# Forgetting values by four query tiles in one bank, low probabilities by half-width products: one change to a hybrid decoder trunk

## The chip, the cores and the metric

The kernel runs on one core of a Trainium2 chip. The metric is the device time of one execution in microseconds (us), taken as the median of several. TensorE is called PE in the profile (its weight loads PEld), VectorE DVE, ScalarE ACT, GpSimd POOL, and SP is the queue that issues the transfers.

## The reference

Two layers work on 1024 tokens of 1024 channels, in float32. Layer 0 mixes by pooling over windows of 2, 4, 8 and 16 tokens and by a 4-head attention into 256 memory tokens. Layer 1 uses the same kind of memory attention beside a "forgetting" attention with 16 heads of 64 channels. Each layer ends in an output projection and a layer norm. The change is about the forgetting attention:

```python
def shared_kv(x, w_kv_shared, b_forget):
    h = x @ w_kv_shared
    k = h[..., :D_MAIN]...; v = h[..., D_MAIN:2 * D_MAIN]...
    log_f = jax.nn.log_sigmoid(h[..., 2 * D_MAIN:] + b_forget)
    return k, v, jnp.cumsum(log_f, axis=1)

# for each block of 128 queries
logits = jnp.einsum('bqhd,bkhd->bhqk', qi, k) * scale
logits = logits + (ci[..., :, None] - cum_k[:, :, None, :])
p = jax.nn.softmax(jnp.where(mask, logits, -jnp.inf), axis=-1)
out = jnp.einsum('bhqk,bkhd->bqhd', p, v)
```

## The kernel before

Products in float32 precision are made of parts. A projection ("slab", 128 output channels by 1024 tokens) takes for each of its two halves of 512 tokens 24 products: 8 blocks of input channels by three terms, high by high and twice high by low. Each half accumulates in one PSUM bank and is then read by ACT and DVE (`evac`). `slab` is a generator that gives up control after each product (line 213), so that its products can be used as filling between others. PSUM has eight banks here: `pj` 3 (slabs), `L` 2 (logits), `T` 2 (exponentials and transposes), `O` 1 (values). PE's order is written out by hand (`manual_schedule(engines={PE})`); the other engines' order comes from a scheduler.

The **forgetting attention** (`fox`) goes over 16 heads, and in each over 8 query tiles of 128 queries from the last (i = 7, with 1024 keys) to the first (i = 0, with 128 keys): 128 steps. A step does this:

- `probs` (lines 789 to 818): the logits of the tile in one or two parts of up to 512 keys, two products each, in an `L` bank (line 197). DVE adds the gates' row R and takes the running extreme (line 807), ACT makes the exponentials into a `T` bank (line 815).
- `halves` (lines 833 to 838), one step later: ACT makes float16 high probabilities (line 836), DVE the low ones (line 837).
- `turn` (line 846): one transposing transfer turns both halves of the tile, into a tile of its own out of the pool of six `T` tiles in SBUF.
- `values`, LAG = 5 steps later and for two query tiles together (every second step): for each tile i and key block j one product with high and one with low probabilities, both with the stationary 128 x 128 tile that holds 64 columns of V's high part and 64 of its low part. Both tiles accumulate in the one `O` bank. ACT (line 862) and DVE (line 863) then add the two halves of partitions and scale.
- `pair_out` (lines 868 to 874): after the second head of a pair POOL multiplies the output by the gate in four pieces and SP writes it to memory (`y1d`).
- `fill.pump`: filling (projections of the next pair of heads, gates) by a budget. `SHARE` says how the filling that is left is spread over the eight steps of a head; before, it is even.

Ahead of `fox`, `start_units` interleaves the first pair's K and Q slabs (`own`) with the projection of the first values and of the gates' logits (`v_first`, line 685), the chain of small DVE operations for the gates (`forget_gates`: cumulative sum by products in lines 716 and 718, a transpose in line 722, a write of the rows to memory), and the next pair's slabs (`following`). `forget_rows` reads a row of gates back for each head.

`mem_kv` makes keys and values of the memory: eight projections for each layer, each of 24 products with 256 columns into a `pj` bank; their weights are split into high and low parts by `split_w`. With `low[0]` set that is done by POOL alone (lines 162 to 164), otherwise by ACT and DVE (lines 154, 155, 159).

`OutProj` is the output projection: `open` takes four banks for two token tiles, `products` (line 442) gives its products, `norm` (lines 489 to 507) reads the banks. Its first part (`early`) is filling at the end of `fox`.

## Time and profile before

| | |
|---|---|
| median of three runs | 1231.65 us (1231.56 to 1234.4) |
| the profiled execution | 1232.92 us, its span 1231.2 us |
| mean granted clock of PE | 0.996 |
| busy: PE / DVE / ACT / POOL | 1205.1 / 800.0 / 709.0 / 226.2 us |
| values products of the forgetting attention | 1152, busy 75.1 us |
| forgetting attention | about 653 to 1115 us of the span |

Busy time of PE is the union of its matmuls with modelled ends; matmuls overlap, so a mean length (220 ns) is longer than the time from one start to the next. In a table of stretches each engine has its busy us and, in brackets, the number of its instructions; then come the granted clock, the transfer engines' share and GB/s. In the list of waits stand the total us, the count and the longest. In a row of groups stand the busy time, the mean ns of one, and the idle time just ahead with what ended it.

### The profile page before, as it was taken

What the parts mean: (1) busy time and instruction counts of PE and PEld (TensorE: products, weight loads), DVE (VectorE), ACT (ScalarE), POOL (GpSimd) and SP (SyncE); (2) the same over time, 40 slices, a digit from 0 to 9 for tenths busy, and PEclk for the clock granted to TensorE, in tenths of its full rate; (3) what the DMA queues carried; (4) which work ended last, traced back from release to release, by engine and by line L of the source; (5) the groups of instructions that cost most, each with busy time, mean ns of one, the idle gap of its engine ahead of it and who ended that gap; (6) DMA issues with size and microseconds to landing.
All of it is one profiled execution on the core that took longest, in us unless ns stands there. A gap on an engine that the chain in (4) does not pass through costs nothing. (4 is left out here: it accounts for less than half of the span.)

```text
span 1231.2 us, 20033 instructions
## 1 busy us (share of the span) xinstructions
PE 1205.1 (98%) x7018; PEld 762.4 (62%) x7018; DVE 800.0 (65%) x1901; ACT 709.0 (58%) x1495; POOL 226.2 (18%) x360
## 2 busy tenths in 40 slices
PE   8999999999999999999998999999999999999996
PEld 4567665555556657566775666666666666655553
DVE  6544776376555458267455888778877888775643
ACT  7566765373532238477334777767776777785210
POOL 2000000000000000000003444444434434550000
PEclk9999999999999999999999999999999999999998
DMA  6333443232453335234516678878777888996430
GB/s 226 117 103 95 120 122 136 94 120 95 144 193 117 103 103 188 61 87 110 184 41 158 143 175 184 185 161 193 172 175 180 179 181 201 229 218 203 165 109 35
DMA packets 267414, 178.68 MB, mean 145 GB/s; under 512 B 212272, under 2 KB 225712, under 8 KB 267312
## 3 DMA queue, kind: packets, MB, share of 16 engines
q1 hardware_dynamic: 267312, 177.40, 53.7%
q8 instruction: 55, 0.90, 0.3%
q14 instruction: 47, 0.39, 0.1%
HBM read 94.97 MB, written 22.61 MB: 96 GB/s over the span
## 5 line engine op out<-in xcount | busy, mean ns | idle before, releaser
L213 PE MATMUL pj<-A,w 128*128 128x512 bf16 (+1 forms) x2928 | 698.7, 393 | 1.9 <-ACT A L154 1.0
L213 PEld LDWEIGHTS <-w 128*128 128x128 bf16 x1984 | 175.4, 98 | 213.2 <-issue 42.7
L213 PEld LDWEIGHTS pj<-A,w 128*128 128x128 f32 x976 | 179.5, 189 | 44.5 <-ACT A L154 2.6
L815 ACT ACTIVATE T<-MK,s 128x512 f32<-128x512 f32 x192 | 110.7, 577 | 49.2 <-DVE s L807 37.3
L837 DVE SCALAR_TENSOR_TENSOR P<-T,s,P 128x512 f16<-128x512 f32 x192 | 111.7, 613 | 33.3 <-ACT P L836 31.6
L836 ACT ACTIVATE P<-T,s 128x512 f16<-128x512 f32 x192 | 102.6, 576 | 50.5 <-issue 21.1
L155 DVE TENSOR_TENSOR w<-raw,w 128x512 bf16<-128x512 f32 x106 | 74.3, 702 | 83.5 <-PE pj L213 50.4
L442 PEld LDWEIGHTS <-T 128*128 128x128 bf16 x736 | 70.8, 98 | 86.6 <-issue 3.7
L197 PE MATMUL L<-B,B 128*128 128x512 f32 (+3 forms) x384 | 109.1, 387 | 7.6 <-DVE s L807 6.7
L157 POOL TENSOR_SCALAR A<-A 128x512 bf16<-128x512 f32 (+1 forms) x20 | 17.4, 884 | 464.4 <-ACT A L154 464.4
L197 PEld LDWEIGHTS L<-B,B 128*128 128x128 f32 x384 | 70.3, 189 | 35.5 <-DVE s L807 18.0
L154 ACT CAST w<-raw 128x512 fp32r<-128x512 f32 x106 | 65.4, 617 | 36.1 <-PE pj L213 25.1
L807 DVE CUSTOM_DVE_ANT_0 MK<-L,R 128x512 f32<-128x512 f32 (+3 forms) x128 | 72.8, 569 | 10.8 <-PE L L197 3.7
L197 PEld LDWEIGHTS <-V 128*128 128x128 f16 x1152 | 67.5, 98 | 18.1 <-issue 8.2
L197 PE MATMUL O<-T,V 128*128 128x128 f16 x1152 | 75.1, 220 | 1.6 <-DVE G L863 1.0
L155 DVE TENSOR_TENSOR T<-T,T 128x1024 bf16<-128x1024 f32 x23 | 28.1, 1221 | 73.7 <-ACT T L154 36.8
L163 POOL TENSOR_TENSOR w<-raw,w 128x512 bf16<-128x512 f32 x54 | 70.1, 1298 | 24.4 <-PE pj L213 22.8
L799 POOL TENSOR_SCALAR_AFFINE_SELECT R<-R 128x128 f32<-128x128 f32 x128 | 41.1, 327 | 163.4 <-DVE s L807 131.4
L159 ACT CAST w<-w 128x512 bf16<-128x512 f32 x106 | 65.6, 618 | 7.2 <-PE pj L213 5.6
L159 ACT CAST T<-T 128x1024 bf16<-128x1024 f32 (+1 forms) x39 | 37.0, 957 | 42.0 <-PE L L442 35.6
L154 ACT CAST T<-T 128x1024 fp32r<-128x1024 f32 x23 | 24.1, 1047 | 53.0 <-DMA T<-y1d 26.9
L442 PE MATMUL pj<-B,T 128*128 128x512 bf16 (+1 forms) x186 | 48.7, 392 | 0.0
(238 smaller groups left out, 1698.8 us busy)
## 6 DMA issues: line engine op xcount, KB each, us to landing
raw<-in_win_dram SPq DMA_DIRECT2D x96, 256.0 KB, 2.8
raw<-in_wout_dram SPq DMA_DIRECT2D x40, 256.0 KB, 2.9
B<-B SPq DMA_DIRECT2D x32, 256.0 KB, 4.2
R<-cumd SPq DMA_DIRECT2D x16, 512.0 KB, 4.2
y0d<-Y SPq DMA_DIRECT2D x12, 512.0 KB, 2.6
T<-y0d SPq DMA_DIRECT2D x12, 512.0 KB, 3.8
T<-y1d SPq DMA_DIRECT2D x11, 512.0 KB, 3.8
raw<-in_wmk_dram SPq DMA_DIRECT2D x16, 256.0 KB, 2.6
```

The lines of the kernel that those rows point to most:

```text
L154: pin(nc.scalar.copy(hi, src))
L155: pin(nc.vector.tensor_tensor(lo[0], src, hi.bitcast(F32), ALU.subtract))
L159: nc.scalar.copy(lo[1], hi.bitcast(F32))
L163: nc.gpsimd.tensor_tensor(lo[0], src, hi.bitcast(F32), ALU.subtract)
L197: nc.tensor.matmul(acc, a, b, start=i == 0, stop=i == len(terms) - 1)
L213: nc.tensor.matmul(acc, a, b, start=start, stop=stop)
L442: nc.tensor.matmul(acc, y, w, start=c == 2 and j == firsts[id(acc)], stop=c == 1 and j == lasts[id(acc)])
L799: nc.gpsimd.affine_select(R[:, qs], R[:, qs], [[-1, P]], ALU.is_ge, -NEG, base=0, channel_multiplier=1).ins
L807: nc.vector.tensor_tensor_reduce(p[:, lo:up], lg, R[:, lo:up], 1.0, top, ALU.add, ALU.min, m[:, n : n + 1])
L815: nc.scalar.activation(e, p[:, lo:up], AF.Exp, bias=top, scale=-1.0, accum_out=sums[:, n, hd % 2, i : i + 1],)
L836: nc.scalar.activation(pair[:, lo:up], e, AF.Copy, scale=r)
L837: nc.vector.scalar_tensor_tensor(pair[:, L + lo : L + up], e, r, pair[:, lo:up], ALU.mult, ALU.subtract)
```

## The change

- `values` takes four query tiles (i = 7 to 4, then 3 to 0) together, in one `O` bank of 512 columns. First come all high products as before; then all low products, with a stationary tile of only the 64 columns of V's high part, whose result goes in turn to partitions 0 to 63 and 64 to 127. The product of low probabilities with V's low part is no longer formed. Each bank is begun once (`start` on the first product only). The number of products and of weight loads on PE stays the same (7010 and 4873).
- The turned probabilities of a head lie in five tiles in place of eight (`HOMES`). `pair_out` gives up control after each piece and is continued step by step, all four pieces after the head's last call.
- PSUM: `L` 3, `pj` 2. The products of the pooling map take `L`; the output projection's banks go by a list in turn.
- `SHARE` is uneven: (1.4, 3.1, 2.9, 2.6, 1.6, 2.2, 2.1, 1.9).
- `start_units`: 24 products of `own` ahead of `v_first` in place of 48; 27 in place of 33 between the last transposes of V and the cumulative sum; nine after it in both; then 60 in place of 30 ahead of the first logits.
- In layer 1, the second half of each memory projection's weights is split by POOL.

```diff
-SHARE = (1,1,1,1,1,1,1,1)
+SHARE = (1.4, 3.1, 2.9, 2.6, 1.6, 2.2, 2.1, 1.9)
+HOMES = ((4, 14), (3, 10), (4, 8), (4, 0), (3, 0), (2, 0), (1, 0), (0, 0))
...
-    def slab(pieces_dram, XH, XL, evac, banks=("pj", 3)):
+    def slab(pieces_dram, XH, XL, evac, banks=("pj", 2)):
...
             for pc in range(2):
+                low[0] = l == 1 and pc == 1
                 a, b = split_w(w_dram[pc], [P, 4, P])
+                low[0] = False
...
-        def open(self, banks=(("pj", 3),) * 2 + (("L", 2),) * 2):
-            accs = [ps([P, NH], *bank) for bank in banks]
+        def open(self, sp):
+            pj, l, t, o = ("pj", 2), ("L", 3), ("T", 2), ("O", 1)
+            turned = ((pj, pj, l, l), (t, t, l, o)) if self.l else ((pj, pj, l, l), (l, o, pj, pj), (l, l, l, o))
+            accs = [ps([P, NH], *bank) for bank in turned[sp % len(turned)]]
...
-                    acc = ps([P, NH], "pj", 3)
+                    acc = ps([P, NH], "L", 3)
...
-            yield from islice(own, 48)
+            yield from islice(own, 24)
             yield from v_first()
             gates = forget_gates()
             next(gates)
             for _ in v_turned():
                 yield from islice(own, 6)
+            yield from islice(own, 27)
+            next(gates)
+            yield from islice(own, 9)
+            next(gates)
             yield from own
-            yield from islice(following, 9)
-            next(gates)
-            yield from islice(following, 9)
-            next(gates)
-            yield from islice(following, 30)
+            yield from islice(following, 48)
...
-                lg = ps([P, NH], "L", 2)[:, : up - lo]
+                lg = ps([P, NH], "L", 3)[:, : up - lo]
...
-            pt[hd, i] = T([P, 2 * ST, P], F16)
-            nc.sync.dma_start_transpose(pt[hd, i][:, :n, :], two[:, : n * P])
+            home, at = HOMES[i]
+            if at == 0:
+                homes[home] = T([P, 2 * ST, P], F16)
+            pt[hd, i] = homes[home][:, at : at + n, :]
+            nc.sync.dma_start_transpose(pt[hd, i], two[:, : n * P])
...
-            acc = ps([P, 2 * P], "O", 1)
-            for i in (2 * c, 2 * c + 1):
-                mm3(
-                    acc[:, (i % 2) * P : (i % 2) * P + P],
-                    [
-                        (v[:, b, 2 * j : 2 * j + 2, :].rearrange("p e d -> p (e d)"), pt[hd, i][:, e * (i + 1) + j, :])
-                        for j in range(i + 1) for e in range(2)
-                    ],
-                )
+            acc = ps([P, NH], "O", 1)
+            blocks = [(i, j) for i in range(4 * c + 3, 4 * c - 1, -1) for j in range(i + 1)]
+
+            def cols(i):
+                return slice((i % 4) * P, (i % 4 + 1) * P)
+
+            for n, (i, j) in enumerate(blocks):
+                nc.tensor.matmul(
+                    acc[:, cols(i)], v[:, b, 2 * j : 2 * j + 2, :].rearrange("p e d -> p (e d)"), pt[hd, i][:, j, :],
+                    start=n == 0, stop=False, skip_group_check=True,
+                )
+            for n, (i, j) in enumerate(blocks):
+                half = slice(64 * (n % 2), 64 * (n % 2) + 64)
+                nc.tensor.matmul(
+                    acc[half, cols(i)], v[:, b, 2 * j, :], pt[hd, i][:, i + 1 + j, :],
+                    start=False, stop=n >= len(blocks) - 2, skip_group_check=True,
+                )
...
-            oc = o[own, c * 2 * P : (c + 1) * 2 * P]
+            oc = o[own, c * NH : (c + 1) * NH]
...
-        def pair_out(pr, c, o, g):
-            for k in {1: (3, 2, 1), 0: (0,)}.get(c, ()) if g is not None else ():
+        def pair_out(pr, o, g):
+            for k in (3, 2, 1, 0) if g is not None else ():
                 cols = slice(k * 2 * P, (k + 1) * 2 * P)
                 nc.gpsimd.tensor_tensor(o[:, cols], o[:, cols], g[:, cols], ALU.mult)
-            if c == 0:
-                nc.sync.dma_start(y1d[pr // 4, :, pr % 4, :], o)
+                yield
+            nc.sync.dma_start(y1d[pr // 4, :, pr % 4, :], o)
...
-                    if older and older[1] % 2 == 0:
-                        values(older[0], older[1] // 2, older[2])
-                        if older[0] % 2:
-                            pair_out(older[0] // 2, older[1] // 2, older[2], gs.get(older[0] // 2))
+                    if older and older[1] % 4 == 0:
+                        values(older[0], older[1] // 4, older[2])
+                        if older[0] % 2 and older[1] == 0:
+                            finished = pair_out(older[0] // 2, older[2], gs.get(older[0] // 2))
+                    next(finished, None)
```

More of the change, by code (lines that the diff above doesn't have):

```diff
@@ L469, in rest @@
                 if c == 2:
-                    accs[sp] = self.open((("T", 2), ("T", 2), ("pj", 3), ("O", 1))) if 0 in accs and sp == 1 else self.open()
+                    accs[sp] = self.open(sp)
                 src, (yh, yl) = T([P, 4, 2 * P], F32), halved(T, [P, 4, 2 * P])
@@ L559, in slab_of @@
                     first[d] if g == 0 else win[0, 2 * g + d], XH, XL,
-                    lambda cols, acc: nc.scalar.copy(us[d][:, cols], acc), ("L", 2) if g == 0 and d == 1 else ("pj", 3),
+                    lambda cols, acc: nc.scalar.copy(us[d][:, cols], acc), ("L", 3) if g == 0 and d == 1 else ("pj", 2),
                 )
@@ L640, in trunk_kernel @@
         flog = fg[:, 0, :]
+        tr = G((P, 2, P))
+        tri, ones = tr[:, 0, :], tr[:, 1, :]
+        nc.gpsimd.memset(ones, 1.0)
+        nc.gpsimd.affine_select(tri, ones, [[1, P]], ALU.is_ge, 0.0, base=0, channel_multiplier=-1)
         def values_of(u):
@@ L678, in v_first @@
             for s in range(ST):
-                acc = ps([P, NH], "pj", 3)
+                acc = ps([P, NH], "pj", 2)
                 terms = []
```

15 lines of the change are left out of this document (6 added, 9 removed).

## The prediction

> **What bounds the kernel now.** I read the page's first part, then the busy time by stage, then what TensorE waits for, then the groups and the order of TensorE's instructions around the forgetting attention.
>
> ```profile
> span 1231.2 us, 20033 instructions
> PE 1205.1 (98%) x7018; PEld 762.4 (62%) x7018; DVE 800.0 (65%) x1901; ACT 709.0 (58%) x1495; POOL 226.2 (18%) x360
> ```
> ```profile
> core 0: us, PE busy (x) PEld busy (x) DVE busy (x) ACT busy (x) POOL busy (x), PEclk, DMA share, GB/s
> ...
> 450.00:480.00 30.00, 27.82 (x200) 21.53 (x200) 24.34 (x53) 19.91 (x40) 1.23 (x2) 1.00 0.42 144
> ...
> 653.00:664.00 11.00, 7.90 (x28) 4.10 (x27) 5.28 (x14) 4.07 (x9) 3.19 (x6) 0.84 0.85 215
> 664.00:780.00 116.00, 114.62 (x745) 75.67 (x744) 94.69 (x277) 84.99 (x204) 51.16 (x86) 1.00 0.74 165
> 780.00:900.00 120.00, 119.15 (x799) 79.67 (x798) 96.01 (x280) 84.94 (x199) 52.78 (x86) 1.00 0.80 185
> 900.00:1000.00 100.00, 99.39 (x667) 66.28 (x664) 80.79 (x234) 73.24 (x171) 41.81 (x70) 1.00 0.75 172
> 1000.00:1030.00 30.00, 27.96 (x181) 17.32 (x179) 23.46 (x73) 21.85 (x54) 10.81 (x20) 1.00 0.96 193
> 1030.00:1115.00 85.00, 83.73 (x523) 53.60 (x522) 65.36 (x160) 63.94 (x138) 42.15 (x58) 1.00 0.91 225
> ```
> ```profile
> PE L L197 <- DVE s L807: 6.7, 13, 2.9
> PE pj L197 <- DVE s L501: 1.6, 1, 1.6
> ...
> PE O L197 <- DVE G L863: 1.0, 2, 0.7
> ...
> PE O L197 <- DMA T<-P: 0.6, 1, 0.6
> ```
>
> TensorE is busy for 98% of the span: the time is the length of its own stream plus a few holes. Only two things can move it: a shorter stream, or fewer holes. The holes that the change can reach are 2.2 us in 450:480 (the second layer's memory keys), 3.1 us in 653:664 with a granted clock of 0.84 (the first forgetting tiles), and in 664:1115, the forgetting attention, (1.38 + 0.85 + 0.61 + 2.04 + 1.27) = 6.2 us. Most of them are waits of the logits for the vector engine to read a bank (6.7 us in 13 waits). DVE is busy there for 360 of 451 us (0.80): it is next in line, but not the bound.
>
> **The values products: the main term.**
>
> ```profile
> L197 PE MATMUL O<-T,V 128*128 128x128 f16 x1152 | 75.1, 220 | 1.6 <-DVE G L863 1.0 <-DMA T<-P 0.6
> ...
> L197 PEld LDWEIGHTS <-V 128*128 128x128 f16 x1152 | 67.5, 98 | 18.1 <-issue 8.2 <-DMA T<-P 1.4
> ```
> ```profile
> 700.80 1.85 PE L197 MATMUL O<-T,V 128*128 128x128 f16 x30
> ```
>
> One call of 30 products takes 1.85 us, of which the last one's own length is 0.22: (1.85 - 0.22) / 29 = 56 ns from start to start. All 1152 make 64.5 us of stream. The changed kernel still issues 1152. The 576 with high probabilities stay as they are. The 576 with low probabilities use a 64-column stationary tile and write partitions 0 to 63 and 64 to 127 in turn; they take 576 x 56 ns = 32.3 us now. No instruction in this trace uses half the array's columns, so I bound it.
>
> Lower end: two neighbours in different halves run side by side, and a pair takes 56 ns: 288 x 56 ns = 16.1 us go. Upper ends: the halves run one after the other, 0 us; or the weight load shows. The nearest rows for a load that sets the pace are the f32 products with little to stream:
>
> ```profile
> 642.36 0.46 PE L716 MATMUL O<-G,G 128*128 128x128 f32 x2 [0.87 <-DVE G L708]
> 642.66 1.63 PE L718 MATMUL O<-G,G 128*128 128x112 f32 x14
> 644.14 2.10 PE L213 MATMUL pj<-A,w 128*128 128x512 bf16 x9
> 646.57 0.33 PE L722 MATMUL T<-ident,G 128*128 128x128 f32 x1 [0.32 <-DVE G L719]
> 646.73 6.78 PE L213 MATMUL pj<-A,w 128*128 128x512 bf16 x30
> 653.15 1.28 PE L197 MATMUL L<-B,B 128*128 128x512 f32 x4
> 654.27 2.22 PE L213 MATMUL pj<-A,w 128*128 128x512 f32 x9
> 659.39 0.73 PE L197 MATMUL L<-B,B 128*128 128x512 f32 x2 [2.90 <-DVE s L807]
> ```
> ```profile
> L718 PEld LDWEIGHTS O<-G,G x14: 192/192/193, 642.5 to 644.0; 128*128 128x128 f32 x14
> ```
>
> Those 14 have streams of 112 columns down to 16 and still go at (1.63 - 0.26) / 13 = 105 ns each: a slow 128-column load. If the 64-column loads cost that much, (105 - 56) x 576 = 28 us come on top; if half as much, 53 ns each, loads in series keep 56 ns and nothing is won. I take 65 ns a pair, so 288 x (112 - 65) = -13.5, rounded to **-13 us**. It lies near the lower end because today's loads of 98 ns already hide completely behind a pitch of 56: the nearest row has more than one load under way.
>
> The Trainium skill (TensorEngine Tiling (Array Packing), Key Properties) says that different tiles load and multiply in parallel, which by itself gives the -16; its section Restrictions says that column tiling switches the fast weight load off, which is the case of 53 ns by the row above. No run here shows either yet.
>
> Going from full-width products to half-width ones and back happens twice in each of the 32 calls: 64 changes. No such change is in the trace. Its price lies between 0 and an emptied array with a bare load: a product alone lasts 220 ns in place of 56, and the load is 98, so at most 0.26 us each or 16.8 us. I take 0.08, half of the 164 ns of the emptying, as the rows show no stop where f16 and f32 follow each other: **+5 us**. The skill's same section says that a change of the tiling mode drains TensorE, which speaks for a price above 0.
>
> Half as many calls also mean 32 evacuations of 512 columns in place of 64 of 256, and the O bank is asked for every fourth step, not every second. That saves DVE and ACT some busy time off the path; the 1.0 us wait for L863 belongs to the holes below. The transposes of probabilities keep their number; only their tiles are packed, and each is still read four or more steps after its issue (128 steps in 451 us: 14 us).
>
> **The start.** Before, 30 products of projection stand between the gates' transpose (646.57) and the first logits; these then wait 2.9 us for their bank, since the vector engine starts on them only when the row of gates has come. The clock falls to 0.84 over 11 us, worth 1.8 us. After, 60 products (60 x 6.78 / 30 = 13.6 us) lie there, and DVE's first logits came 12.1 us after that transpose:
>
> ```profile
> 646.22 0.29 DVE L719 COPY G<-O 128x128 f32<-128x128 f32 x1
> ...
> 658.63 0.69 DVE L807 CUSTOM_DVE_ANT_0 MK<-L,R 128x512 f32<-128x512 f32 x1 [2.45 <-DMA R<-cumd]
> ```
>
> So 3.1 + 1.8 go. But ahead of the cumulative sum (642.36, which already waits 0.87) stand 27 products in place of 33, 1.3 us less cover: **-3.5 us**, between -4.9 and -1.
>
> **Holes in the forgetting attention.** Three logits banks let the logits run one bank further ahead, and SHARE gives the steps with long rows more projection work. Of 6.2 us I take **-3.5**; ends -6.2 and 0, since DVE still has to read all the logits.
>
> **Memory keys, layer 2.** Half the weight splits go to POOL:
>
> ```profile
> L163 POOL TENSOR_TENSOR w<-raw,w 128x512 bf16<-128x512 f32 x54 | 70.1, 1298 | 24.4 <-PE pj L213 22.8 <-PE L L197 0.7
> L162 POOL TENSOR_SCALAR w<-raw 128x512 fp32r<-128x512 f32 x54 | 33.9, 628 | 78.1 <-DVE G L704 43.9 <-PE pj L213 25.6 <-issue 8.6
> L164 POOL TENSOR_SCALAR w<-raw 128x512 bf16<-128x512 f32 x54 | 33.4, 618 | 0.0
> ```
> ```profile
> 480.89 0.41 DVE L290 TENSOR_REDUCE s<-pj 128x1 f32<-128x256 f32 x1
> ...
> 480.90 4.27 PE L197 MATMUL pj<-T,w 128*128 128x256 bf16 x36
> ...
> 484.60 0.48 DVE L298 SCALAR_TENSOR_TENSOR MK<-pj,s,MK 128x256 f16<-128x256 f32 x1
> ```
>
> POOL needs 0.63 + 1.30 + 0.62 = 2.5 us for one, TensorE 24 x 4.27 / 36 = 2.8 us for one projection: POOL keeps up, DVE loses eight subtractions, and the 2.2 us of waits mostly go. Against it stands the third slab bank: the projection read at 480.89 is released at 485.1, while two banks want it back one projection after 480.90, at 483.7. That is 1.4 us, and perhaps as much again for the next. I take **-1**, between -2.2 and +2. In the forgetting stage a slab's half lasts 24 products of 0.22 us (6.78 us for 30 at 646.73) with other work between, so two slab banks are covered there; in the first layer likewise.
>
> **The end.** Pair 7's four gatings run behind the last call, where before one did:
>
> ```profile
> 1108.57 0.73 POOL L872 TENSOR_TENSOR G<-G,G 128x256 f32<-128x256 f32 x1 [4.90 <-DVE G L863]
> ```
> ```profile
> 1109.33 0.33 SPq L874 DMA_DIRECT2D y1d<-G  x1
> ...
> 1112.79 0.52 SPq L472 DMA_DIRECT2D T<-y1d  x1
> ```
> ```profile
> 1120.28 1.04 ACT L154 CAST T<-T 128x1024 fp32r<-128x1024 f32 x1 [3.62 <-DMA T<-y1d]
> ```
> ```profile
> 1125.46 0.81 PE L442 MATMUL pj<-R,T 128*128 128x512 f32 x2
> ```
>
> The write moves 3 x 0.73 = 2.2 us later, and behind it on SP's queue the last weight fetches, the norm's rows and the read of pair 4 to 7. That read's high half is ready at 1121.3 and used at 1125.5: 4.1 us hide it, so **0**, at worst +2 if TensorE gets there sooner.
>
> **Sum.** The profiled execution took 1232.9 us (span 1231.2 and 1.7 around it): 1232.9 - 13 + 5 - 3.5 - 3.5 - 1 = 1216.9. The median of the runs shown lies 1.3 below that execution: **1216 us**.
>
> **Rivals.** (1) The loads set the pace: low products stay at 56 ns, the rest as above: 1231.65 - 3 = 1229. For it: the 105 ns of L718, halved. Against: the loads of two halves touch different columns. Chance 0.15.
>
> (2) Slower: the halves work one after the other and the array empties at every change of width, 64 x 0.26 = +16.8 against -8 from start, holes and keys: 1240. It needs both parts; with no gain from the halves it decides from 8 / 64 = 0.125 us per change, with the gain of 13 never below 0.33. For it: a lone product lasts 220 ns. Against: nothing in the trace stops at a change of type. This is also the case in which the change does not do what it says. Chance 0.16.
>
> (3) DVE takes over: its 360 us stand in a stage that shrinks from 451 to 439 us (0.82), and half of that stage's net gain of 11.5 returns as waits of logits for L807: 1222. For it: those waits are already the largest. Against: SHARE fills those steps. Chance 0.12.
>
> **How the numbers follow.** The forecast has 0.57. All lower ends together give -16.1 - 4.9 - 6.2 - 2.2 = -29.4, so 1202; all of them at once is unlikely, and the range starts at 1204. Above, it must take in rival 1 and most of rival 2: 1238. About 0.3%, 3.7 us, is what a measurement here can tell from no change, so faster means below 1228. Faster: the forecast, rival 3 and half of rival 1, less a little for a dear drain: 0.74. Same: the other half of rival 1: 0.09. Slower: rival 2: 0.17.
>
> **What would show it.** Right: low products at 28 to 40 ns from start to start, so that the group of values products falls from 75 to about 62 us; no 2.9 us wait at the first logits and a clock of 1.00 there; L807 waits below 3 us. Wrong: low products at 56 ns or more, holes of 0.1 to 0.3 us where the width changes, new waits for pj banks at the memory values or at the late gates, or a longer wait than 2.2 us for L708.

## The result, and the profile after

The kernel with the change takes 1236.65 us (median of 20 runs, 1233.63 to 1239.59), the one before 1234.22 us (20 runs, 1231.25 to 1236.83). The ratio is 1.0022, with a 95% interval of 1.0012 to 1.0031: the change costs 2.4 us. The profiled execution has a span of 1234.4 us, before 1231.2.

The first part of the page, and the same stretches as before (busy us and number of instructions of PE, PEld, DVE, ACT, POOL, then clock, transfer share, GB/s):

```profile
span 1234.4 us, 19993 instructions
PE 1197.7 (97%) x7018; PEld 755.2 (61%) x7018; DVE 789.2 (64%) x1861; ACT 691.1 (56%) x1447; POOL 251.5 (20%) x384
```
```profile
450.00:480.00 30.00, 25.86 (x176) 19.41 (x175) 21.65 (x39) 11.18 (x25) 19.92 (x19) 0.98 0.43 137
...
653.00:664.00 11.00, 11.00 (x52) 6.83 (x51) 5.30 (x11) 3.92 (x8) 5.48 (x8) 1.00 0.75 215
664.00:780.00 116.00, 115.20 (x765) 75.52 (x764) 94.44 (x278) 86.16 (x201) 51.57 (x87) 1.00 0.84 176
780.00:900.00 120.00, 114.28 (x787) 75.16 (x784) 92.98 (x268) 81.65 (x188) 53.02 (x87) 0.99 0.79 177
900.00:1000.00 100.00, 98.38 (x646) 63.64 (x640) 78.10 (x226) 69.37 (x160) 42.16 (x71) 1.00 0.77 174
1000.00:1030.00 30.00, 28.82 (x232) 19.95 (x231) 25.01 (x80) 23.02 (x56) 11.97 (x20) 1.00 0.94 204
1030.00:1115.00 85.00, 78.19 (x475) 47.82 (x474) 64.33 (x146) 62.41 (x134) 41.10 (x56) 0.96 0.91 222
```

TensorE has 7.4 us less to do (1197.7 in place of 1205.1) and the span is 3.2 us longer: over 10 us of new holes. The start is clean (11.00 of 11.00 us, clock 1.00). New holes stand in the memory keys (4.1 us idle in 450:480, before 2.2), in 780:900 (5.7, before 0.85) and in 1030:1115 (6.8, before 1.3). What TensorE waits for there:

```profile
PE pj L214 <- DVE B L755: 5.2, 2, 2.6
PE pj L447 <- DVE G L243: 3.9, 1, 3.9
PE L L198 <- DVE s L812: 3.1, 4, 1.1
PE pj L198 <- POOL w L165: 2.3, 2, 2.1
PE pj L214 <- POOL w L163: 1.9, 1, 1.9
PE pj L198 <- POOL w L164: 1.8, 2, 1.4
PE O L867 <- DMA T<-P: 1.4, 2, 1.1
```

The logits' waits fell from 6.7 to 3.1 us, but 2.9 us of that is the one wait at the first logits; behind it they went from 3.8 to 3.1. The five rows for slabs, output projection and memory keys are new: a slab waits for a bank that DVE still reads, the output projection for the bank of a late gate, the memory keys for weights that POOL splits. Between the same points of the program in both traces, the stretch from the memory keys to the first logits grew from 192.8 to 198.7 us, that from the first to the last logits fell from 434.2 to 425.2, and that from the last logits to the last product grew from 133.1 to 139.5: +5.9 - 9.0 + 6.4 = +3.3, the difference of the spans (3.2) within rounding.

The waits are not the whole loss. TensorE's granted clock falls with three of them, here with the last (the stretch, then as above):

```profile
1093.00:1101.00 8.00, 6.98 (x19) 4.53 (x20) 7.88 (x10) 7.32 (x14) 4.78 (x4) 0.57 0.79 231
```

It is 0.50 for 3.4 us behind the waits that end at 477.7 and 785.1, and for 6.8 us, from 1093.2 on, with the wait that ends at 1094.0; no fall follows the wait of 2.6 us that ends at 896.9. The kernel before has one such fall, 3.4 us behind the wait at the first logits. Up to half of these times is lost: 6.8 us, before 1.7. From 440 us on, TensorE's waits add up to 22.2 us, before 11.7. So 10.5 us more of waits and up to 5.1 us of clock stand against values products that are busy 13.2 us less (75.1 to 61.9).

### The profile page after: what moved, and what is told of

Its sections match the earlier page's. It is cut to its first block, busy times and chain, and to the rows that moved or that the text cites. A ratio compares the mean times of both kernels' runs of the same rounds, so it can differ in the third digit from the quotient of the medians.

```text
span 1234.4 us, 19993 instructions
## 1 busy us (share of the span) xinstructions
PE 1197.7 (97%) x7018; PEld 755.2 (61%) x7018; DVE 789.2 (64%) x1861; ACT 691.1 (56%) x1447; POOL 251.5 (20%) x384
## 5 line engine op out<-in xcount | busy, mean ns | idle before, releaser
L214 PE MATMUL pj<-A,w 128*128 128x512 bf16 (+1 forms) x2928 | 691.5, 392 | 10.4 <-DVE B L755 5.2
L156 DVE TENSOR_TENSOR w<-raw,w 128x512 bf16<-128x512 f32 x98 | 70.0, 714 | 79.8 <-PE pj L214 50.3
L158 POOL TENSOR_SCALAR A<-A 128x512 bf16<-128x512 f32 (+1 forms) x20 | 17.7, 901 | 433.3 <-ACT A L155 433.3
L155 ACT CAST w<-raw 128x512 fp32r<-128x512 f32 x98 | 60.5, 617 | 44.8 <-PE pj L214 27.3
L164 POOL TENSOR_TENSOR w<-raw,w 128x512 bf16<-128x512 f32 x62 | 81.9, 1320 | 12.8 <-PE pj L214 10.2
L804 POOL TENSOR_SCALAR_AFFINE_SELECT R<-R 128x128 f32<-128x128 f32 x128 | 41.0, 326 | 181.9 <-DVE s L812 116.8
L160 ACT CAST w<-w 128x512 bf16<-128x512 f32 x98 | 60.6, 618 | 7.3 <-PE pj L214 5.6
L160 ACT CAST T<-T 128x1024 bf16<-128x1024 f32 (+1 forms) x39 | 37.0, 957 | 42.8 <-PE O L447 16.2
L163 POOL TENSOR_SCALAR w<-raw 128x512 fp32r<-128x512 f32 x62 | 40.2, 648 | 80.5 <-PE pj L214 64.3
L198 PE MATMUL pj<-T,w 128*128 128x256 bf16 (+1 forms) x384 | 47.0, 284 | 4.5 <-POOL w L165 2.3
L447 PE MATMUL L<-B,T 128*128 128x512 bf16 (+1 forms) x168 | 42.7, 385 | 0.0
```

What stands on the lines that cost most here:

```text
L155: pin(nc.scalar.copy(hi, src))
L156: pin(nc.vector.tensor_tensor(lo[0], src, hi.bitcast(F32), ALU.subtract))
L160: nc.scalar.copy(lo[1], hi.bitcast(F32))
L164: nc.gpsimd.tensor_tensor(lo[0], src, hi.bitcast(F32), ALU.subtract)
L198: nc.tensor.matmul(acc, a, b, start=i == 0, stop=i == len(terms) - 1)
L214: nc.tensor.matmul(acc, a, b, start=start, stop=stop)
```

## The experiments

The differences below are between a kernel's median and that of the kernel before in the same study. In the expectations a letter stands for the place where a theory puts the loss: A the two slab banks and A' the split on POOL, B the products themselves, C the spread of the filling, D the collected calls of four tiles, E the order of the casts at the end. The expectations of the last two studies name theirs in full.

| kernel | median us | to before, us | ratio (95%) |
|---|---|---|---|
| the change | 1236.65 | +2.4 | 1.0022 (1.0012, 1.0031) |
| three_banks | 1233.88 | -0.8 | 0.9996 (0.9982, 1.0011) |
| no_pool_split | 1231.77 | -2.9 | 0.9982 (0.997, 0.9995) |
| both_undone | 1231.79 | -2.9 | 0.9982 (0.9965, 0.9998) |
| full_width | 1241.95 | +7.3 | 1.0061 (1.0046, 1.0076) |
| both_even | 1234.02 | +0.1 | 0.9996 (0.9986, 1.0007) |
| values_alone | 1238.27 | +4.3 | 1.0038 (1.0026, 1.0051) |
| one_half | 1241.87 | +7.9 | one run |
| by_tile | 1243.72 | +9.8 | one run |
| tail_pool | 1226.05 | -7.9 | 0.9939 (0.992, 0.9959) |
| two_tiles | 1231.52 | -2.5 | 0.9982 (0.9972, 0.9992) |
| two_tiles_start | 1227.13 | -6.9 | 0.9945 (0.9933, 0.9957) |
| combined | 1227.32 | -6.7 | 0.9947 (0.9934, 0.996) |
| spread | 1231.69 | -2.7 | 0.9979 (0.9968, 0.9991) |
| packed_gated | 1239.68 | +5.3 | 1.0043 (1.0027, 1.006) |
| spread_tail | 1223.50 | -10.9 | 0.9914 (0.9899, 0.993) |
| packed_only | 1240.69 | +6.5 | 1.0052 (1.0036, 1.0067) |
| gated_only | 1232.38 | -1.8 | 0.9985 (0.9975, 0.9995) |

### First study: which part of the change costs

`three_banks` gives the slabs their third bank back (logits two; the output projection's list of banks and the pooling map's bank go back with it), `no_pool_split` lets ACT and DVE split the memory weights again, `both_undone` does both, and `full_width` puts the low products back on a 128-column stationary tile (with V's low part, so it computes a little more).

```diff
 three_banks
-    def slab(pieces_dram, XH, XL, evac, banks=("pj", 2)):
+    def slab(pieces_dram, XH, XL, evac, banks=("pj", 3)):
...
-                lg = ps([P, NH], "L", 3)[:, : up - lo]
+                lg = ps([P, NH], "L", 2)[:, : up - lo]
...
 no_pool_split
-                low[0] = l == 1 and pc == 1
+                low[0] = False
 full_width
...
-                    acc[half, cols(i)], v[:, b, 2 * j, :], pt[hd, i][:, i + 1 + j, :],
+                    acc[:, cols(i)], v[:, b, 2 * j : 2 * j + 2, :].rearrange("p e d -> p (e d)"), pt[hd, i][:, i + 1 + j, :],
```

three_banks: 

> The changed kernel with the banks of before: three for slabs, two for logits. Theory A (two slab banks give back what the half-width products save: in the changed kernel's trace TensorE waits for a slab bank 5.2 us at L755, 3.9 at L243 and some 2 at L294, L301 and L744): these 11 us go, the waits of logits for L812 grow from 3.1 to 5 or 6, so about 1227 beside 1234 of before. Theory B (the saved stream cannot show, because DVE and ACT set the pace of the forgetting stage): 1233 or more, waits of the same sum in other places. Theory C (SHARE packs the filling so densely that the readers fall behind whatever the banks): waits for L755 stay, 1233 or more.

no_pool_split: 

> The changed kernel with all weights of the second layer's memory projections split by ACT and DVE, as before. Theory A': POOL's chain of three operations (2.5 us for one half) is too slow where TensorE needs one in 2.8 us; in the changed kernel TensorE waits 4.1 us for POOL there, before it waited 2.2 for DVE: 2 to 3 us less, 1234. Rival: the holes there come from the two slab banks, and 1236 to 1237 stay.

both_undone: 

> Both: three slab banks and two logits banks, and no split by POOL. Theory A with A': the two gains add, about 1224 (0.992 of before). Theory B: 1233 or more. Theory C: 1231 or more, with waits for L755.

full_width: 

> The changed kernel with the low products again on a full 128-column stationary tile, everything else kept. If the stream of TensorE sets the time here: the group of values products goes back from 62 to 75 us less the 64 changes of width (95 ns each, 6 us), so +10 us, about 1247. If the holes swallow what the products save (theory B): 1237, the holes smaller by the same 10 us.

The split on POOL costs 4.9 us (1236.65 to 1231.77) with two slab banks, and 2.1 us with three (1233.88 to 1231.79). The banks cost 2.8 us while the split is there and nothing without it (1231.77 against 1231.79). In part that is because another wait takes the place of theirs: behind the last logits, where the changed kernel waits 3.9 us for the late gate's bank, `three_banks` and `both_undone` wait 3.1 and 2.8 us for a cast (T, L160, below). So theory A, the banks as the whole loss, fell. And the products of half width are worth something: with `full_width` in their place the kernel is 5.3 us slower still, about half of the 10 us expected if the stream alone set the time.

Why POOL was no help, in the changed kernel's order of POOL at the second layer's memory keys, and TensorE beside it:

```profile
469.16 1.05 POOL L163 TENSOR_SCALAR w<-raw 128x512 fp32r<-128x512 f32 x1
470.33 1.82 POOL L164 TENSOR_TENSOR w<-raw,w 128x512 bf16<-128x512 f32 x1
472.12 1.06 POOL L165 TENSOR_SCALAR w<-raw 128x512 bf16<-128x512 f32 x1
473.14 1.05 POOL L163 TENSOR_SCALAR w<-raw 128x512 fp32r<-128x512 f32 x1
474.16 1.19 POOL L158 TENSOR_SCALAR A<-A 128x512 bf16<-128x512 f32 x2
475.32 1.69 POOL L164 TENSOR_TENSOR w<-raw,w 128x512 bf16<-128x512 f32 x1
476.99 0.61 POOL L165 TENSOR_SCALAR w<-raw 128x512 bf16<-128x512 f32 x1
```
```profile
477.66 6.25 PE L198 MATMUL pj<-T,w 128*128 128x256 bf16 x40 [2.06 <-POOL w L165]
```

The first of these splits has POOL to itself and still takes 4.0 us (469.16 to 473.18), as each operation is longer here than in the rows of the forecast; those of the split from 477.56 are as short as there (0.61, 1.28, 0.62). No run shows why. In the second, two casts of activations (L158) stand in POOL's queue between the parts: it runs 473.1 to 477.6, not 2.5 us, and TensorE waits 2.06 us for its last part.

### Second study: the values and the start by themselves

`both_even` is `both_undone` with an even SHARE; `values_alone` has the old start besides, so it is the kernel before with the values' part of the change (and two small edits ahead of the forgetting attention: the pooling map's bank, and an earlier place for the triangle of the gates' sums; it reaches the first logits at 653.4 us, the kernel before at 653.2). `one_half` puts all low products into partitions 0 to 63; `by_tile` alternates high and low products by query tile, with 256 changes of width in place of 64.

```diff
 one_half
-                half = slice(64 * (n % 2), 64 * (n % 2) + 64)
+                half = slice(0, 64)
...
 by_tile
...
+            for i in range(4 * c + 3, 4 * c - 1, -1):
+                for j in range(i + 1):
+                    nc.tensor.matmul(
+                        acc[:, cols(i)], v[:, b, 2 * j : 2 * j + 2, :].rearrange("p e d -> p (e d)"), pt[hd, i][:, j, :],
...
+                for j in range(i + 1):
+                    half = slice(64 * (j % 2), 64 * (j % 2) + 64)
...
```

both_even: 

> Three slab banks, two logits banks, no split by POOL, and SHARE even as before; what is left of the change is the values products, the packed tiles, the gating in four pieces after the head and the start's order. Theory C (the uneven SHARE makes TensorE arrive too early at banks, at the gates' weights from POOL and at the output projection): about 1224, 7 below the run with SHARE uneven (1231.8), with the waits at the end (2.8 us for POOL, 2.8 for ACT) and those for the logits smaller. Theory D (those waits come from the values themselves: their calls now come in two lumps of 52 and 20 products and the gating follows late): 1231 to 1233, the same waits.

values_alone: 

> The kernel before with nothing changed but the values (four query tiles in one bank, half-width low products, packed tiles, gating in four pieces after the last call). If the half-width products save 16 us of stream and 64 changes of width cost 6, and nothing else is lost: 1234.7 - 10 = 1225. If the lumps lose it again in holes (theory D): 1231 to 1235. If the start's order is worth its 3.5 us, this is 3.5 above the run with three slab banks, no POOL split and even SHARE.

one_half: 

> The changed kernel with all low products in partitions 0 to 63, none in the other half. If neighbours in different halves run side by side: the low products, 4 and 53 ns from start to start in turn in the changed kernel, go at 53 to 56 ns each, and the group is 16 us longer; the changes of width stay at 64. If the half width alone were the gain, 28 ns each would stay.

by_tile: 

> The changed kernel with high and low products in turn for each query tile: 256 changes of width in place of 64. If a change costs 95 ns over the pitch, 192 more are 18 us of stream, some of it hidden where TensorE waits anyway: 10 to 18 us longer. If the 150 ns seen at a change are only an artefact of how starts are stamped, the time stays within 2 us.

The rows of the two groups of products, high (L867, L869) and low (L873, L876), in the changed kernel, in `one_half` and in `by_tile`:

```profile
L867 PE MATMUL O<-T,V 128*128 128x128 f16 x576 | 39.4, 223 | 1.5 <-DMA T<-P 1.4
L873 PE MATMUL O<-T,V 128*64 128x128 f16 x576 | 22.5, 224 | 0.0
```
```profile
L873 PE MATMUL O<-T,V 128*64 128x128 f16 x576 | 38.4, 221 | 0.0
```
```profile
L869 PE MATMUL O<-T,V 128*128 128x128 f16 x576 | 54.2, 221 | 0.0
L876 PE MATMUL O<-T,V 128*64 128x128 f16 x576 | 42.1, 229 | 0.0
```

Products in alternate halves run side by side: 22.5 us busy, 38.4 when all go to one half. In `by_tile` the busy times are longer mostly because each short run's last product lasts 0.22 us in place of a pitch, and the other group has begun by then; they are not stream. One call with its neighbour shows the pitch and the price of a change of width:

```profile
1087.22 1.62 PE L867 MATMUL O<-T,V 128*128 128x128 f16 x26
1088.78 0.92 PE L873 MATMUL O<-T,V 128*64 128x128 f16 x26
1089.63 0.50 PE L447 MATMUL pj<-MK,B 128*128 128x512 f32 x1
```

26 low products: (0.92 - 0.22) / 25 = 28 ns from start to start, 56 ns a pair. 26 high ones at 56 ns start their last at 1087.22 + 1.40 = 1088.62; the first low one starts 0.16 us later, the last low one (1088.78 + 0.70 = 1089.48) is followed 0.15 us later. So a change costs about 0.15 - 0.056 = 0.09 to 0.10 us, and all 64 about 6 us. The Trainium skill (TensorEngine Tiling (Array Packing), Key Properties) says that tiles run in parallel and that a change of mode drains TensorE. The first agrees with the 28 ns. For the second the rows show the price of 0.09 to 0.10 us alone, which is less than the 164 ns that the forecast set for emptying the array; whether it empties they do not show.

But `one_half`, with 15.9 us more in the stream, is only about 5 us slower than the changed kernel (by one run), and `by_tile`, with 192 more changes of width or some 18 us, about 7; the values' part alone makes the kernel before 4.3 us slower, more than any theory had allowed it. The stream did get shorter, and something else took more than that. `both_even` against `values_alone`, 4.3 us, is the start; an uneven SHARE brings another 2.2 (`both_even` to `both_undone`; 3.0 if each is set against its own runs of before), so C fell. The 1234.0 us of `both_even` lie above what D said, too.

### Third study: half width without the collected calls, and the end

`two_tiles` is the kernel before with low products of half width, in its own calls of two tiles (so 128 changes of width) and with nothing else of the change; `two_tiles_start` adds the changed start. `tail_pool` is `both_undone` with the low cast of the output projection's first input block on POOL. `combined` is the changed kernel with the weights' split undone, the memory values' projections in L banks, that cast on POOL, and the early output projection's banks in another order.

```diff
 two_tiles (against the kernel before)
-            for i in (2 * c, 2 * c + 1):
-                mm3(
...
+            blocks = [(i, j) for i in (2 * c + 1, 2 * c) for j in range(i + 1)]
...
+                half = slice(64 * (n % 2), 64 * (n % 2) + 64)
+                nc.tensor.matmul(
+                    acc[half, (i % 2) * P : (i % 2) * P + P], v[:, b, 2 * j, :], pt[hd, i][:, i + 1 + j, :],
...
 tail_pool (against both_undone)
-                hi_lo(yh, yl, src)
+                hi_lo(yh, yl, src, aside=self.accs is not None and (sp, c) == (0, 0))
 combined (against the change)
-                low[0] = l == 1 and pc == 1
+                low[0] = False
...
-            acc = ps([P, NH], "pj", 2)[:, :NMEM]
+            acc = ps([P, NH], *banks)[:, :NMEM]
...
-            turned = ((pj, pj, l, l), (t, t, l, o)) if self.l else ((pj, pj, l, l), (l, o, pj, pj), (l, l, l, o))
+            turned = ((l, l, pj, pj), (t, t, l, o)) if self.l else ((pj, pj, l, l), (l, o, pj, pj), (l, l, l, o))
...
-                hi_lo(yh, yl, src)
+                hi_lo(yh, yl, src, aside=self.accs is not None and (sp, c) == (0, 0))
```

tail_pool: 

> The run with three slab banks and no POOL split in the memory projections (1231.8), and at the end of the forgetting stage the low cast of the first block of the output projection's input on POOL in place of ACT. Theory E (the scheduler of the changed kernel has put this cast on ACT behind the casts of weights that come late, so that TensorE stands 2.8 to 4.6 us and its clock falls): the wait for L160 goes, 3 to 5 us less, 1227 to 1229. Rival (the block itself comes late, because its tiles are held by the packed probabilities): the wait stays with POOL or the transfer in ACT's place, 1231 to 1232.

two_tiles: 

> The kernel before with half-width low products and nothing else: values still by two query tiles, with all high and then all low products in a call, 128 changes of width. Stream: 15.5 us less for the halves, 128 x 95 ns = 12 us more for the changes, so -3: 1231. If the lumps of four tiles made the holes of the run with the values alone (theory D, 1238): no new holes here, 1229 to 1233, and the end stage as long as before. If half-width products make holes in themselves: 1236 or more.

two_tiles_start: 

> The same with the changed order of the start. The order was worth 4 us between the two runs that differ in it alone (1234.0 and 1238.3): 4 less than the run without it, about 1227. If it was worth that only together with the lumps: no difference.

combined: 

> The changed kernel without its three losses: no POOL split in the memory projections (-5 by the run that did so), the memory values' projections in the three logits banks, idle there (the last 2 us between memory keys and first logits), the first output block's low cast on POOL, and that block's products in the logits banks first, so that the slab banks are wanted 2 us later. Three logits banks, two slab banks and the uneven SHARE stay. Theory: 1236.6 - 5 - 2 - 2 = 1227 or 1228, 0.5% under the kernel before. If two slab banks cost as much wherever the waits are moved: 1231 or 1232.

`two_tiles` is faster than before, `values_alone` slower, although the first has twice as many changes of width. With the start it is at 1227.1. And one cast on another engine wins 5 us (`both_undone` -2.9, `tail_pool` -7.9). `combined`, which keeps two slab banks, comes to 1227.3 as expected; 1.7 us of the wait for the late gate's bank stay in it. The waits of `both_even` and `tail_pool` show which cast it is:

```profile
PE L L198 <- DVE s L813: 8.4, 18, 0.8
PE pj L448 <- ACT T L160: 4.6, 1, 4.6
```
```profile
PE L L198 <- DVE s L813: 4.7, 9, 0.8
PE pj L214 <- POOL w L163: 2.9, 1, 2.9
```

The 4.6 us wait is for that cast (T, L160). In `both_even` ACT makes the high cast at 1096.44 and the low one only at 1103.72; before, they stand at 1099.34 and 1100.81. Between them ACT's queue casts late weights, with waits of 0.81 and 0.39 us until they land:

```profile
1096.44 1.04 ACT L155 CAST T<-T 128x1024 fp32r<-128x1024 f32 x1
1098.81 1.34 ACT L155 CAST MK<-raw 128x512 fp32r<-128x512 f32 x2 [0.81 <-DMA raw<-in_wout_dram]
...
1103.72 1.04 ACT L160 CAST T<-T 128x1024 bf16<-128x1024 f32 x1
```

The wait is paid again in clock: over 1102 to 1110 us it is 0.57 in `both_even`, and 1.00 from 1090 to 1110 in `tail_pool`.

### Fourth and fifth study: what lies between two tiles and four

From `two_tiles` to `values_alone` three edits to the forgetting attention are left: the packing of the turned tiles (`HOMES`), the gating in four pieces after the last call, and the call of four tiles. `packed_gated` adds the first two to `two_tiles`; `packed_only` and `gated_only` add one. `spread` is `values_alone`, but the high products of two tiles are issued every second step, where the kernel before has its calls, and only the low ones wait for all four. `spread_tail` is the same in `tail_pool`.

```diff
 spread (against values_alone)
-            acc = ps([P, NH], "O", 1)
-            blocks = [(i, j) for i in range(4 * c + 3, 4 * c - 1, -1) for j in range(i + 1)]
+            if i0 % 4 == 2:
+                held[0] = ps([P, NH], "O", 1)
+            acc, c = held[0], i0 // 4
+            blocks = [(i, j) for i in (i0 + 1, i0) for j in range(i + 1)]
...
+            if i0 % 4:
+                return
+            blocks = [(i, j) for i in range(4 * c + 3, 4 * c - 1, -1) for j in range(i + 1)]
 packed_only (against two_tiles)
-            pt[hd, i] = T([P, 2 * ST, P], F16)
+            home, at = HOMES[i]
+            if at == 0:
+                homes[home] = T([P, 2 * ST, P], F16)
+            pt[hd, i] = homes[home][:, at : at + n, :]
...
 gated_only (against two_tiles)
-            for k in {1: (3, 2, 1), 0: (0,)}.get(c, ()) if g is not None else ():
+            for k in (3, 2, 1, 0) if g is not None else ():
...
+                yield
```

spread: 

> The kernel with the values change alone, but the high products of two query tiles are issued every second step, at the place where the kernel before has its calls; only the low products wait for all four tiles, so that the changes of width stay 64. Theory D1 (the collected call of four tiles makes the holes: steps without values products have too little TensorE work between logits): the waits of logits for a bank fall from 12.0 us to about 7 and the time from 1238.3 to 1230 to 1233. Theory D2 (what packs the turned tiles or puts the gating late makes them): the time stays at 1237 to 1239. Theory D3 (only the last call matters, by where the scheduler puts the cast of the first output projection block): the forgetting stage stays at 432 us and only the end falls, from 139.7 to about 135.

packed_gated: 

> The kernel before with half-width low products by two tiles, and of the rest of the values change only the packing of the turned tiles and the gating in four pieces after the head's last call. D1: as two tiles without these, 1231.5 within 1, logits' waits 6 to 7 us, end 132. D2: towards 1238, logits' waits about 12 us. D3: forgetting stage as before, end 132 if the last call alone decides, 136 to 140 if the late gating does.

spread_tail: 

> The kernel with all of the change but the banks and the GpSimd split, and the first output projection block's low cast on GpSimd, now with the high products issued every second step as above. D1: the 64 changes of width and the filled steps go together: 2 to 4 us under 1226.1, so 1222 to 1224. D2 and D3: 1226 within 1.5.

packed_only: 

> The kernel before with half-width low products by two tiles and the turned tiles packed, the gating as before. Theory P (the packing alone frees a T tile in SBUF earlier, so the scheduler may place the read of the first output projection block and its high cast ahead of the last exponential in ACT's order; ACT then waits 4 to 5 us for that read and everything of the last tiles is late): 1238 to 1241, a wait of ACT for the read of about 4.9 us near 1090, last logits to end 148 to 153 us. Theory Q (the late gating delays the writes and reads at the end): 1231.5 within 1.5, last logits to end 142 to 144 us.

gated_only: 

> The same with the gating in four pieces after the head's last call, the turned tiles as before. P: 1231.5 within 1.5, no wait of ACT for that read above 0.6 us. Q: 1236 to 1241.

The packing alone costs 9.2 us (1231.52 to 1240.69), the gating less than one. In the profiles 8.4 us of it stand after the last logits (their start to the last product: `two_tiles` 132.0 us, `gated_only` 132.5, `packed_only` 140.4): TensorE waits 5.2 us there (3.9 and 1.3), and the clock is 0.57 over 1097 to 1105. It is a matter of order. SP reads the first input block of the output projection into a T tile of the same pool. With five T tiles for a head in place of eight that read starts at 1090.15 in `packed_only` (before: 1095.60), and the scheduler has put its cast ahead of the last tile's exponentials. ACT of `packed_only`, then of the kernel before:

```profile
1096.54 1.04 ACT L155 CAST T<-T 128x1024 fp32r<-128x1024 f32 x1 [5.89 <-DMA T<-y1d]
1097.49 0.36 ACT L816 ACTIVATE T<-MK,s 128x128 f32<-128x128 f32 x1
...
1106.36 1.04 ACT L160 CAST T<-T 128x1024 bf16<-128x1024 f32 x1
```
```profile
1099.34 1.05 ACT L154 CAST T<-T 128x1024 fp32r<-128x1024 f32 x1 [0.40 <-DMA T<-y1d]
...
1100.81 1.04 ACT L159 CAST T<-T 128x1024 bf16<-128x1024 f32 x1
```

ACT stands 5.89 us before a transfer, and behind it in its queue wait the exponentials of the last query tile and the casts for the output projection. With four-tile calls the high cast comes behind the exponentials, but the low one follows 7.6 us after it in the changed kernel (1096.97 and 1104.60) and 6.6 us in `values_alone`, not 1.5.

In the changed kernel itself TensorE does not wait for that cast. Its 3.9 us there go back to POOL. The kernel before has the mask of the last query tile (L799, which hides the later keys in the gates' row) ahead of a late gate's multiplication (L882) on POOL; in the changed kernel the scheduler has put it (L804) behind one (L899), which waits for a read from memory. The changed kernel by time, then POOL of the kernel before:

```profile
1088.48 0.73 POOL L899 TENSOR_TENSOR R<-R,G 128x256 f32<-128x256 f32 x1 [5.85 <-DMA R<-y1d]
1089.16 0.29 POOL L804 TENSOR_SCALAR_AFFINE_SELECT R<-R 128x128 f32<-128x128 f32 x1
1089.49 0.29 DVE L812 CUSTOM_DVE_ANT_0 MK<-L,R 128x128 f32<-128x128 f32 x1 [3.50 <-POOL R L804]
1089.82 0.37 ACT L820 ACTIVATE T<-MK,s 128x128 f32<-128x128 f32 x1 [3.28 <-DVE s L812]
...
1091.77 0.58 ACT L242 ACTIVATE G<-pj 128x512 f32<-128x512 f32 x1
...
1093.29 0.67 DVE L243 SCALAR_TENSOR_TENSOR G<-G,pj 128x512 f32<-128x512 f32 x1
...
1094.02 1.22 PE L447 MATMUL pj<-V,B 128*128 128x512 f32 x2 [3.89 <-DVE G L243]
```
```profile
1087.01 0.73 POOL L799 TENSOR_SCALAR_AFFINE_SELECT R<-R 128x128 f32<-128x128 f32 x1
...
1091.43 2.02 POOL L882 TENSOR_TENSOR R<-R,G 128x256 f32<-128x256 f32 x2 [2.40 <-DMA R<-y1d]
```

DVE, then ACT stand for the mask, and behind them in their queues come the two operations that free the late gate's bank. `tail_pool` has the same order on POOL (a wait of 5.31 us) and three slab banks, and TensorE does not wait there. No run changed that order alone.

`spread` is 6.6 us faster than `values_alone`. Logits' waits of `values_alone`, of `spread` and of `two_tiles`, from the memory keys to the end:

```profile
PE L L198 <- DVE s L813: 12.0, 24, 1.8
```
```profile
PE L L198 <- DVE s L813: 9.0, 10, 2.8
```
```profile
PE L L197 <- DVE s L807: 6.5, 10, 3.4
```

With collected calls the waits go from 10 to 24: in a step without values products the logits come again before DVE has read their bank. The packing does not do this: `packed_gated` is as slow as D2 said (1239.7), but its logits wait 6.3 us in 10 waits. With the uneven SHARE there is less of it: 4.7 us in 9 waits in `tail_pool`, 2.9 in 7 in `spread_tail`. `spread` has 10 waits again, though longer ones than D1 expected (9.0 us, not 7). Of its 6.6 us, 3.4 lie between the first and the last logits (431.9 to 428.5), which is D1, and 3.1 behind them (139.7 to 136.6), which is D3: the low cast now follows the high one after 2.0 us. Where the cast waits no more, spreading brings 2.6 us (`tail_pool` to `spread_tail`), about what D1 alone is worth. `spread_tail` takes **1223.5 us**, 0.9% less than the kernel before, and beats both kernels.

## Why the prediction was wrong

The forecast was 1216 us, 15.7 below the median it started from; the result is 2.4 above its own. The range holds it, and so does the margin of 0.3% called the same, but the sign was wrong. By its own steps, with steps of the ladder from the runs:

- **Products: right.** Busy time of the values products 39.4 + 22.5 = 61.9 us, predicted about 62. A change of width 0.09 to 0.10 us, taken at 0.08. Rival 1 (loads set the pace) and the mechanism of rival 2 (halves in series, 0.26 per change) are refuted: 28 ns per low product.
- **Start: right.** Predicted -3.5; 4.3 and 4.4 us in two pairs of kernels. The wait for the gates' sum is 0.8 us (0.87 before), so the thinner cover cost nothing.
- **Holes in the forgetting attention: half right.** The prediction read the logits' 6.7 us as lying inside the attention's 6.2 us of holes, but 2.9 of them belong to the first logits, which the start had already counted. Inside, these waits fell from 3.8 to 3.1 only, while other waits raised the holes of 664:1115 from 6.2 to 16.1 us in the changed kernel. Of the -3.5, SHARE brings 2.2 to 3.0, and the banks nothing:
- **"Two slab banks are covered there": failed.** The term was 0, and the changed kernel has 5.2 + 3.9 us of waits for them; `three_banks`, without these, waits 5.4 us for logits (3.1 in the change) and 3.1 for the late cast. The prediction named new waits for these banks "at the late gates" as a sign of being wrong, but gave them no price. The reasoning counted 24 products of cover for a slab's half, but not how long DVE takes to release it, nor that the late gates' banks are wanted by the output projection:

```profile
782.88 0.68 DVE L755 SCALAR_TENSOR_TENSOR B<-pj,B 64x512 fp32r<-64x512 f32 x1
784.28 0.69 DVE L755 SCALAR_TENSOR_TENSOR B<-pj,B 64x512 fp32r<-64x512 f32 x1 [0.33 <-ACT B L754]
```
```profile
785.12 0.93 PE L214 MATMUL pj<-A,w 128*128 128x512 f32 x3 [2.62 <-DVE B L755]
```

- **Memory keys: wrong sign.** Predicted -1, measured +4.9 to +5.3 for the split with two slab banks, +2.1 with three. The step that failed is "POOL keeps up": it took the 2.5 us of a split from rows of the forgetting attention, where at the memory keys one took 4.0 us with POOL to itself, and it took POOL's queue for free (4.5 us with two casts in between). Of the 6.1 us between the profiles of the change and of `no_pool_split` 4.0 lie there; 3.8 lie behind the last logits, and 1.4 go the other way between.
- **Tiles "only packed": failed, the largest miss of the runs with two-tile calls.** The prediction gave the packing no cost, because the transposes keep their number. It did not ask what else is allocated from the same pool and when that would start. Added to two-tile calls it costs 9.2 us. How much of the changed kernel's loss is the packing's, no run shows.
- **"The end: 0": failed for the same reason.** It asked whether the late write delays the read; `gated_only` shows under 1 us for that. The loss is in the orders of ACT and POOL, which the diff does not show. The stretch from the last logits grew by 6.4 us: in the changed kernel a wait of 3.9 us, which goes back to POOL, and the clock's fall behind it; with three slab banks the wait for the late cast, 5 us with its clock by `tail_pool`.
- **The clock: left out.** The prediction priced the clock once, at the start, where it was won as said (1.8 us). It put nothing on what new waits would do to it: three falls, up to 6.8 us lost, 5.1 more than before.
- **Calls of four tiles.** The prediction counted half as many calls as a small saving. Without the packing's effect they should save 64 changes, 6 us; from `packed_gated` to `values_alone` it is 1.0: the holes of the collected calls take the rest, and `spread` gets 6.6 back, the cast's place included.
- **Rival 3** (half of a stream gain returns as waits) has the right size for wrong reasons: 15.9 us more stream in `one_half` costs 5, and not because DVE is the bound: TensorE's waits fall from 22.2 to 17.9 us and the clock's loss from 6.8 to 3.4, as the added work fills holes that other waits leave.

The ladder from before to after, in differences to before: two tiles of half width -2.5, packing and gating +7.8, four tiles -1.0, start -4.2, SHARE -3.0, banks 0, POOL +5.3; sum +2.4. The terms of the prediction added to -16, so 18.4 us are missing: 7.8 from packing and gating, 6.3 at the memory keys (+5.3, not -1), 4.5 in the values (-3.5, not -8); start and holes (-7.2, not -7.0) came out as said. Each kernel's difference to before has about 1.5 us on either side, a rung, between two of them, about 2; so four tiles (-1.0) and banks are not told from nothing. The rungs depend on their order: the packing was added to two-tile calls, and the split counts 5.3 with two slab banks. Going down from the change, the same losses were taken away one by one: the split 4.9, the banks 0, the late cast 5.0 to 5.7, the collected high products 2.6 to 3.0, which ends at 1223.5, still 7.5 us above the forecast.

What stays open: the 1.9 us that slabs wait for weights split by POOL (L163) near 1073 us, 2.9 in `tail_pool`, were seen in the four-tile kernels but not taken away by a run. Nor was the packing tried in the full change by itself, or the mask of the last query tile moved ahead on POOL there, at which the 3.9 us for the late gate's bank begin.

## What to carry to other kernels

A bank, a tile pool or an engine's queue taken from one user can be paid by its other users: before costing an edit at nothing, list everything that allocates from that pool or stands in that queue, and how late it releases. Where a scheduler orders the other engines, compare its order before and after around the end of the kernel: a cast placed ahead of the last exponentials cost 9 us in one run here, more than the main gain. Price a new wait of TensorE with the fall of its clock, where a trace shows one. When a shorter stream has to fill the gaps between instructions that wait on another engine, shorten it in place; collecting it into fewer, larger calls opened holes here.

## What the runs showed of the hardware

Two 64-column products in different halves, each with its own weight load, go as a pair in 56 ns, as long as one product of 128 columns. All in one half, they show no loss against full width either: 38.4 us busy, less 0.16 us for the last product of each of 32 calls, is 58 ns for one. A change between 128 and 64 columns costs 0.09 to 0.10 us beyond the usual pitch, in both directions (one call of the changed kernel).

The granted clock fell to 0.50 for 3.4 us behind TensorE's waits of 2.90 us (before), 2.06 and 2.62 us (the change), and for 6.8 us with waits of 3.89 us (the change), 4.55 us (`both_even`) and 3.94 us (`packed_only`). Not every such wait did it: 2.61 us at 896.9 in the change did not.
